# The second layer's modulation vectors: multiplied and summed on VectorE instead of TensorE, in a two-layer diffusion trunk

## Chip, cores and metric

One core of a Trainium2 chip runs the whole program. The metric is device time in microseconds (us) of one execution. Three runs of the kernel before took 1745.84 us at the median (1744.97 to 1749.46). About 0.3% of that, 5.2 us, is what a measurement can tell from no change.

## What is computed

The reference is a trunk of two layers over 256 latent tokens and 256 context tokens of width 1024. In every layer a conditioning vector (one for the latents, one for the context) gives six vectors of width 1024 that shift, scale and gate the tokens:

```python
silu_c, silu_cc = jax.nn.silu(c)[:, None, :], jax.nn.silu(c_ctx)
for i in range(DEPTH):                                   # DEPTH = 2
    m_lat = jnp.split(silu_c @ mod_w[i] + mod_b[i], 6, axis=-1)    # mod_w[i]: 1024 x 6144
    m_ctx = jnp.split(silu_cc @ mod_w[i] + mod_b[i], 6, axis=-1)
    # mixer: pooling | Hyena | differential attention, gated by m_lat[2], m_ctx[2]
    # layer 0: dense SwiGLU on both streams; layer 1: top-2 of 8 experts, latents only
```

So each layer's modulation is the product of a 1024 x 6144 matrix with two vectors. In the second layer the context stream is used only through its first two vectors (shift and scale of the first norm), since the result is the latent stream alone.

## The kernel before

The program runs in stages: loads and the first layer's modulation, the first mixer with its output projection, the dense SwiGLU of the first layer ("the dense stage"), the second mixer, and the routed experts.

**Modulation.** `mod_w` of a layer is cut into 12 tiles `ct` of 512 output columns, and each tile into 4 chunks `q` of 256 rows, loaded as a 128 x 1024 tile `modw` (L345). `modulation_part` (L353) multiplies a chunk on TensorE: the stationary operand is `cvec`, 128 x 32, which holds the two conditioning vectors (the other columns are 0), the moving operand is a 128 x 256 piece of the weights, and four such matmuls, for two row blocks and two column halves, stand side by side in the array. After the fourth chunk, `modulation_row` copies the sum to SBUF on ScalarE (L360), transposes it with two matmuls (L363), and VectorE adds the two halves (L367) and the bias (L369) into `modT`.

The first 10 tiles are done in the early stages. The last two tiles of layer 0 and the 12 tiles of layer 1, 14 x 4 = 56 chunks, are handed out one at a time by `mod_chunk`, as filler in the dense stage.

**The dense stage.** `dense` runs over 22 blocks of hidden width 128. Each takes two projections (gate and up) of 24 matmuls with 512 moving columns: `three` (L272 to L274) multiplies in three parts, since weights and activations are each split into a high and a low half. Calls of `mod_chunk` stand after each projection in `up`, and after each output block in the two first calls of `down`. "Block" below means one such set of 24 matmuls, of a projection or of a down-projection.

**Weights.** `weight` loads a 128 x 1024 tile `raw` (L259), ScalarE makes the high half `wh` (L262), VectorE the low half `wl` (L263). `raw` and `modw` share one ring of 7 buffers; `wh` and `wl` have 4 each. The projections write to one of three PSUM banks `mm`; for each pair ScalarE takes SiLU of one (L890), VectorE multiplies by the other (L891) and makes the low half of the product (L267). For an output block VectorE adds the two gated residuals (L839).

**Order of the work.** The program is written in the order of these loops; a scheduler then sets the order of each engine's queue, and each engine works through its own queue in order. All loads here go through SyncE's queue.

Of the kernel before, what the change touches and what calls it, by code (L numbers as in the profile page):

```python
# [18 lines left out]
F32 = mybir.dt.float32  # L19
# [3 lines left out]
OP = mybir.AluOpType  # L23
AX = mybir.AxisListType

P = 128
D = 1024
KD = D // P
L = 256
# [8 lines left out]
PAD = 8  # L38
# [157 lines left out]
class Trunk:  # L196
# [130 lines left out]
    def conditioning(self):  # L327

        nc = self.nc
        lo = self.par_at["c"][0]  # L330
        both = self.pars[:, lo:lo + 2 * KD]
        sc = self.keep.tile([P, 2 * KD], F32, name="silu_c")
        nc.scalar.activation(sc, both, AF.Exp, scale=-1.0)
        nc.vector.tensor_scalar(sc, sc, 1.0, None, op0=OP.add)
        nc.vector.reciprocal(sc, sc)
        nc.vector.tensor_mul(sc, sc, both)
        self.cvec = self.pre.tile([P, KD, 32], F32, name="cvec")
        nc.gpsimd.memset(self.cvec, 0.0)
        for j in range(2):
            nc.vector.tensor_copy(self.cvec[:, :, j], sc[:, j * KD:(j + 1) * KD])  # L340
# [51 lines left out]
    def mod_chunk(self):  # L392

        if not self.chunks:
            return
        l, ct, q = self.chunks.pop(0)
        if q == 0:
            self.mod_ps = self.sc()
        self.modulation_part(self.mod_ps, q, self.modulation_load(l, ct, q))
        if q == 3:  # L400
            self.modulation_row(l, ct, self.mod_ps, self.aux)

    def mod_chunks_until(self, l, ct):
        while self.chunks and self.chunks[0][:2] < (l, ct):
            self.mod_chunk()
# [1038 lines left out]
```

## Time and profile before

| | |
|---|---|
| median of 3 runs | 1745.84 us (1744.97 to 1749.46) |
| the profiled execution | 1746.36 us, its span 1743.9 us |
| TensorE busy | 1672.5 us (96%) |
| VectorE busy | 608.8 us (35%) |
| ScalarE busy | 444.2 us (25%) |
| GpSimd busy | 29.4 us (2%) |
| mean granted TensorE clock | 0.991 |

The span runs from the first instruction to the last; 2.46 us of the execution's time lie around it. PE is TensorE's matmul side, PEld its weight loads, DVE VectorE, ACT ScalarE, POOL GpSimd, SP SyncE. A record's duration is from its start to its modelled end; matmuls are pipelined, so the cost of one in a row of them is the distance from start to start. A float32 matmul shows as two records, one of the split halves (fp32r) and a transpose as one.

### The profile page before, as it was taken

The numbers are of one execution on the slowest core, as the hardware profiler recorded it, in microseconds if no ns is written. First come the engines' busy times: TensorE is split into PE (matmuls) and PEld (weight loads), VectorE is DVE, ScalarE is ACT, GpSimd is POOL, SyncE is SP. The second block draws the span as 40 slices with busy tenths as digits, with TensorE's granted clock in tenths as the row PEclk, the third lists the DMA queues.
The fourth block names the chain that finished last, engine by engine and source line by source line (L and its number), as shares of the span: only waits on it lengthen the run. The fifth ranks groups of instructions, "written<-read, shape, count | busy, mean of one in ns | idle before, by whom it ended". The sixth has DMA issues, their size and how long they took to land. (4 is left out here: it accounts for less than half of the span.)

```text
span 1743.9 us, 27710 instructions
## 1 busy us (share of the span) xinstructions
PE 1672.5 (96%) x11718; PEld 1107.2 (63%) x11718; DVE 608.8 (35%) x1352; ACT 444.2 (25%) x866; POOL 29.4 (2%) x38
## 2 busy tenths in 40 slices
PE   6999999999999999999979999999999999999977
PEld 3777568877777777887755555555555555556533
DVE  5645785533332333768740110221103111031103
ACT  4444464422122122546620100110001000010101
POOL 0021000000000000011000000000000000000000
PEclk8999999999999999999989999999999999999999
DMA  8531262455555554532549999999999999999995
GB/s 302 179 107 58 84 255 73 158 157 169 169 164 165 160 165 132 181 109 85 194 166 387 394 390 423 425 382 422 414 402 426 423 424 408 425 424 425 425 425 239
DMA packets 86314, 475.92 MB, mean 273 GB/s; under 512 B 9708, under 2 KB 13069, under 8 KB 43149
## 3 DMA queue, kind: packets, MB, share of 16 engines
q1 hardware_dynamic: 85580, 473.12, 70.4%
q8 instruction: 121, 1.98, 0.4%
q10 hardware_dynamic: 576, 0.52, 0.1%
q14 instruction: 37, 0.30, 0.1%
HBM read 472.55 MB, written 1.05 MB: 272 GB/s over the span
## 5 line engine op out<-in xcount | busy, mean ns | idle before, releaser
L1136 PE MATMUL mm<-mraw,xg 128*64 128x256 f32 x3584 | 407.8, 381 | 16.4 <-DMA mraw<-in_eg_dram 6.7
L1136 PEld LDWEIGHTS mm<-mraw,xg 128*64 128x64 f32 x3584 | 277.9, 137 | 152.8 <-issue 30.3
L272 PE MATMUL mm<-xh,wh 128*128 128x512 f32 (+1 forms) x656 | 240.8, 368 | 0.8 <-ACT wh L262 0.4
L274 PE MATMUL mm<-xh,wl 128*128 128x512 f32 (+1 forms) x656 | 237.6, 363 | 0.3 <-DVE wl L263 0.3
L273 PE MATMUL mm<-xl,wh 128*128 128x512 f32 (+1 forms) x656 | 237.6, 363 | 0.1
L262 ACT CAST wh<-raw 128x1024 fp32r<-128x1024 f32 (+1 forms) x124 | 128.0, 1034 | 362.6 <-PE mm L273 342.4
L263 DVE TENSOR_TENSOR wl<-raw,wh 128x1024 fp32r<-128x1024 f32 (+1 forms) x124 | 149.9, 1211 | 139.8 <-ACT wh L262 138.1
L1153 DVE TENSOR_TENSOR h<-h,mm 128x256 f32<-128x256 f32 x56 | 23.6, 421 | 408.2 <-ACT h L1152 408.1
L272 PEld LDWEIGHTS mm<-xh,wh 128*128 128x128 f32 x656 | 122.9, 188 | 37.0 <-issue 16.5
L274 PEld LDWEIGHTS mm<-xh,wl 128*128 128x128 f32 x656 | 123.2, 188 | 22.0 <-issue 2.2
L273 PEld LDWEIGHTS mm<-xl,wh 128*128 128x128 f32 x656 | 123.1, 188 | 18.9 <-issue 1.5
L1152 ACT ACTIVATE h<-mm 128x256 f32<-128x256 f32 x56 | 21.5, 383 | 415.7 <-PE mm L1136 415.6
L1185 PE MATMUL sc<-mraw,ht 128*64 128x512 f32 x448 | 109.1, 603 | 3.9 <-PEq L1192 1.9
L1185 PE MATMUL mm<-mraw,ht 128*64 128x512 f32 x448 | 108.8, 603 | 3.4 <-DMA mraw<-in_ed_dram 1.5
L1156 DVE TENSOR_TENSOR hx<-hx,sc 64x256 f32<-64x256 f32 x56 | 23.8, 425 | 232.0 <-ACT hx L1155 231.9
L1155 ACT ACTIVATE hx<-sc 64x256 f32<-64x256 f32 x56 | 21.0, 375 | 259.3 <-PE sc L1147 165.5
L1147 PE MATMUL sc<-mraw,xg 128*32 128x256 f32 x1344 | 76.4, 379 | 0.0
L1185 PEld LDWEIGHTS sc<-mraw,ht 128*64 128x64 f32 x448 | 28.9, 136 | 56.3 <-issue 39.4
L1185 PEld LDWEIGHTS mm<-mraw,ht 128*64 128x64 f32 x448 | 29.1, 136 | 52.1 <-issue 42.3
L1147 PEld LDWEIGHTS sc<-mraw,xg 128*32 128x32 f32 x1344 | 43.4, 110 | 29.5 <-issue 1.2
L839 DVE SCALAR_TENSOR_TENSOR x_latents<-mm,modT,x_latents 128x256 f32<-128x256 f32 x40 | 18.6, 481 | 95.7 <-PE mm L274 95.7
L353 PE MATMUL sc<-modw,cvec 128*32 128x256 f32 x576 | 45.0, 396 | 3.0 <-DMA modw<-in_mod_dram 2.9
(330 smaller groups left out, 2004.2 us busy)
## 6 DMA issues: line engine op xcount, KB each, us to landing
mraw<-in_eg_dram SPq DMA_DIRECT2D x112, 1024.0 KB, 14.4
mraw<-in_eu_dram SPq DMA_DIRECT2D x112, 1024.0 KB, 17.9
mraw<-in_ed_dram SPq DMA_DIRECT2D x112, 1024.0 KB, 11.1
modw<-in_mod_dram SPq DMA_DIRECT2D x96, 512.0 KB, 3.8
raw<-in_win_dram SPq DMA_DIRECT2D x40, 512.0 KB, 4.0
raw<-in_fg_dram SPq DMA_DIRECT2D x22, 512.0 KB, 4.6
raw<-in_fu_dram SPq DMA_DIRECT2D x22, 512.0 KB, 4.5
raw<-in_wout_dram SPq DMA_DIRECT2D x16, 512.0 KB, 4.2
```

The source lines that it names most:

```text
L262: nc.scalar.copy(hi, raw)
L263: nc.vector.tensor_sub(lo, raw, hi.bitcast(F32))
L272: mm(ps, w[0], x[0], start=start, stop=False)
L273: mm(ps, w[0], x[1], start=False, stop=False)
L274: mm(ps, w[1], x[0], start=False, stop=stop)
L353: self.nc.tensor.matmul(ps[g:g + 32, :L], self.cvec[:, 2 * q + k], w[:, k * 512 + n * L:k * 512 + (n + 1) * L], start=q == 0, stop=q == 3, ...
L1136: last = mm(pm[MAIN * j:MAIN * (j + 1), i * L:(i + 1) * L], xg[:, k, :MAIN], r, start=k == 0, stop=k == KD - 1, tile_position=(0, MAIN * j))
L1147: mm(px[q:q + EXTRA], xg[:, k, MAIN:], r, start=k == 0, stop=k == KD - 1, tile_position=(0, q))
L1152: nc.scalar.activation(h, pm[:, :L], AF.Silu)
L1153: nc.vector.tensor_mul(h, h, pm[:, L:])
L1156: nc.vector.tensor_mul(hx[64:], hx[64:], px[64:])
L1185: mm(pds[e % 2][n * MAIN:(n + 1) * MAIN], ht[:, c:c + MAIN], r[:, at + n * 512:at + (n + 1) * 512], start=ft == 0 and k == 0, stop=ft == N ...
```

## The change

For layer 1 a chunk no longer goes to TensorE. VectorE multiplies each 128 x 512 half of the chunk by the conditioning value of its row (one value a partition, `silu_c`) and adds it to a running sum: `pz` for the latents, `pa` for the context. The first operation of a tile is a `tensor_scalar` (L421 of the new file), the others are `scalar_tensor_tensor` (L423). For tiles `ct` 0 to 3, which hold shift and scale of the first norm, both streams are summed, for `ct` 4 to 11 the latents alone. After the fourth chunk TensorE sums over the partitions: for each 128 columns of a running sum one matmul with that 128 x 128 piece as the stationary operand and a column of ones as the moving one (L428). VectorE then adds the bias (L433). The tiles `pz` and `pa` take the place of tiles of the same names that the first mixer uses, with one buffer each. Layer 0's chunks stay as they were.

```diff
         nc.vector.tensor_mul(sc, sc, both)
+        self.silu_c = sc
...
         l, ct, q = self.chunks.pop(0)
+        if l == 1:
+            return self.mod_sums(ct, q)
         if q == 0:
             self.mod_ps = self.sc()
...
+    def mod_sums(self, ct, q):
+
+
+        nc = self.nc
+        streams = 2 if ct < 4 else 1
+        if q == 0:
+            wide = [self.temps.tile([P, 2, L + 2 * PAD], F32, name=self.name(n), tag=n, bufs=1) for n in ("pz", "pa")[:streams]]
+            self.sums = [t.rearrange("p s t -> p (s t)")[:, :512] for t in wide]
+        w = self.modulation_load(1, ct, q)
+        for k in range(2):
+            wk = w[:, k * 512:(k + 1) * 512]
+            for j, acc in enumerate(self.sums):
+                c = j * KD + 2 * q + k
+                c = self.silu_c[:, c:c + 1]
+                if q == k == 0:
+                    nc.vector.tensor_scalar(acc, wk, c, None, op0=OP.mult)
+                else:
+                    nc.vector.scalar_tensor_tensor(acc, wk, c, acc, op0=OP.mult, op1=OP.add)
+        if q == 3:
+            ps = self.aux(8)
+            for j, acc in enumerate(self.sums):
+                for b in range(4):
+                    nc.tensor.matmul(ps[:, 4 * j + b:4 * j + b + 1], acc[:, b * P:(b + 1) * P], self.ones[:, 0:1],
+                                     start=True, stop=True)
+            m, mb = self.modT[1][:, 4 * ct:4 * ct + 4], self.par("mod_b1")[:, 4 * ct:4 * ct + 4]
+            for j in range(2):
+                at = 4 * j if streams == 2 else 0
+                nc.vector.tensor_add(m[:, :, j], ps[:, at:at + 4], mb)
```

Three places show how the queues move. The first is TensorE's queue in the dense stage at the end of the first layer-1 tile. Before (`sc` is the bank of the chunks' sum, `aux` that of the transposes, `mm` those of the blocks; xN counts equal instructions):

```order
L273 MATMUL mm_3465<-xl_2647,wh_3461 128x512
L274 MATMUL mm_3465<-xh_2646,wl_3462 128x512
L353 MATMUL sc_3364<-modw_3490,cvec 32x256 x4
L272 MATMUL mm_3510<-xh_2632,wh_3506 128x512
L273 MATMUL mm_3510<-xl_2633,wh_3506 128x512
L274 MATMUL mm_3510<-xh_2632,wl_3507 128x512
L272 MATMUL mm_3510<-xh_2634,wh_3506 128x512
L363 MATMUL aux_3498<-tab_ident,t_710_3496 128x128 x2
L273 MATMUL mm_3510<-xl_2635,wh_3506 128x512
```

The same place in the change:

```order
L273 MATMUL mm_3466<-xl_2647,wh_3462 128x512
L274 MATMUL mm_3466<-xh_2646,wl_3463 128x512
L428 MATMUL aux_3497<-tab_ones,pz_3364 128x1 x4
L428 MATMUL aux_3497<-tab_ones,pa_3365 128x1 x4
L272 MATMUL mm_3514<-xh_2632,wh_3510 128x512
L273 MATMUL mm_3514<-xl_2633,wh_3510 128x512
```

The group of four at the end of every block is gone and so are the two transposes; eight matmuls with one moving column stand behind the fourth block of a tile (four where only the latents are summed), between the last matmul of one block and the first of the next.

The second place is VectorE's queue in the change around the end of that tile's sums and the start of the next tile's (L368 and L370 are the last row of layer 0, L923 is L891 of the file before):

```order
L423 SCALAR_TENSOR_TENSOR pa_3365<-modw_3491,silu_c,pa_3365 128x512
L263 TENSOR_TENSOR wl_3463<-raw_3460,wh_3462 128x1024
L368 TENSOR_REDUCE modT_73<-aux_3327 128x4 x2
L370 TENSOR_TENSOR modT_73<-modT_73,pars 128x8
L923 TENSOR_TENSOR t_690_3372<-t_690_3372,mm_3339 128x512
L263 TENSOR_TENSOR wl_3511<-raw_3508,wh_3510 128x1024
L267 TENSOR_TENSOR v_692_3376<-t_690_3372,v_691_3375 128x512
L263 TENSOR_TENSOR wl_3557<-raw_3554,wh_3556 128x1024
L923 TENSOR_TENSOR t_703_3453<-t_703_3453,mm_3422 128x512
L263 TENSOR_TENSOR wl_3594<-raw_3591,wh_3593 128x1024
L267 TENSOR_TENSOR hy_705_3457<-t_703_3453,hy_704_3456 128x512
L421 TENSOR_SCALAR pz_3539<-modw_3541,silu_c 128x512
```

The last addition to the first tile's sums stands ahead of `wl_3463`, the weights of the block `mm_3466` behind which TensorE sums. The first operation of the next tile writes `pz` again and so stands behind TensorE's sums; ahead of it are the weights of the three blocks that follow those sums.

The third place is VectorE's queue in the first down-projection, where both streams are summed beside the residuals (L871 is L839 of the file before):

```order
L871 SCALAR_TENSOR_TENSOR x_latents<-mm_3691,modT_73,x_latents 128x256
L871 SCALAR_TENSOR_TENSOR x_context<-mm_3691,modT_73,x_context 128x256
L423 SCALAR_TENSOR_TENSOR pz_3716<-modw_3796,silu_c,pz_3716 128x512
L423 SCALAR_TENSOR_TENSOR pa_3717<-modw_3796,silu_c,pa_3717 128x512
L423 SCALAR_TENSOR_TENSOR pz_3716<-modw_3796,silu_c,pz_3716 128x512
L423 SCALAR_TENSOR_TENSOR pa_3717<-modw_3796,silu_c,pa_3717 128x512
L263 TENSOR_TENSOR wl_3807<-raw_3804,wh_3806 128x1024
L423 SCALAR_TENSOR_TENSOR pz_3716<-modw_3835,silu_c,pz_3716 128x512
L871 SCALAR_TENSOR_TENSOR x_latents<-mm_3732,modT_73,x_latents 128x256
L871 SCALAR_TENSOR_TENSOR x_context<-mm_3732,modT_73,x_context 128x256
```

Four multiply-adds stand between the residuals of one block and the next, where before there was only one `wl`. SyncE's queue holds the same loads in the same order as before.

## Rows read from the trace of the kernel before

**Rows 1.** Page, part 1: busy time of TensorE, share, instructions
```profile
PE 1672.5 (96%) x11718; PEld 1107.2 (63%) x11718; DVE 608.8 (35%) x1352; ACT 444.2 (25%) x866; POOL 29.4 (2%) x38
```
**Rows 2.** Windows: length, busy time (instructions) of each engine, clock, DMA share, GB/s
```profile
core 0: us, PE busy (x) PEld busy (x) DVE busy (x) ACT busy (x) POOL busy (x), PEclk, DMA share, GB/s
340.00:380.00 40.00, 40.00 (x201) 29.99 (x200) 13.43 (x20) 11.49 (x15) 0.00 (x0) 1.00 0.47 143
...
660.00:700.00 40.00, 40.00 (x190) 30.82 (x189) 14.23 (x26) 10.77 (x18) 0.00 (x0) 1.00 0.44 129
700.00:850.00 150.00, 144.81 (x805) 114.38 (x803) 115.37 (x244) 85.85 (x170) 12.39 (x16) 1.00 0.44 150
...
1000.00:1200.00 200.00, 196.90 (x1838) 111.82 (x1836) 31.10 (x79) 20.95 (x50) 0.00 (x0) 1.00 0.99 407
...
1400.00:1600.00 200.00, 195.96 (x1738) 113.56 (x1732) 31.39 (x82) 21.63 (x52) 0.00 (x0) 1.00 1.01 421
```
**Rows 3.** Timeline of TensorE in the dense stage, one chunk to the next: start, duration
```profile
384.20 0.39 PE L274 MATMUL mm<-xh,wl 128*128 128x512 f32 x1
384.52 0.64 PE L353 MATMUL sc<-modw,cvec 128*32 128x256 f32 x8
...
385.67 0.39 PE L274 MATMUL mm<-xh,wl 128*128 128x512 f32 x1
385.90 0.39 PE L272 MATMUL mm<-xh,wh 128*128 128x512 f32 x1
...
390.48 0.40 PE L274 MATMUL mm<-xh,wl 128*128 128x512 f32 x1
390.80 0.64 PE L353 MATMUL sc<-modw,cvec 128*32 128x256 f32 x8
```
**Rows 4.** The same timeline around the two transposes of a tile
```profile
398.45 0.40 PE L272 MATMUL mm<-xh,wh 128*128 128x512 f32 x1
398.68 0.38 PE L363 MATMUL aux<-tab_ident,t 128*128 128x128 f32 x2
...
399.37 0.39 PE L272 MATMUL mm<-xh,wh 128*128 128x512 f32 x1
```
**Rows 5.** Groups by line, TensorE, 340 to 705 us: records, busy, mean ns, idle
```profile
L353 PE MATMUL sc<-modw,cvec 128*32 128x256 f32 x416 | 33.2, 391 | 0.0
```
**Rows 6.** Timeline of TensorE, filter stage: matmuls with one moving column (L475)
```profile
64.20 0.95 PE L475 MATMUL sc<-tab_ones,t 128*128 128x1 f32 x8
65.01 0.68 PE L485 MATMUL sc<-k,tab_st 128*128 128x256 f32 x2
```
**Rows 7.** Timeline of TensorE's weight loads at the same place
```profile
63.98 1.08 PEld L475 LDWEIGHTS sc<-tab_ones,t 128*128 128x128 f32 x8
64.98 0.30 PEld L485 LDWEIGHTS sc<-k,tab_st 128*128 128x128 f32 x2
```
**Rows 8.** All records of that line: duration in ns, minimum, median, maximum
```profile
L475 PE MATMUL sc<-tab_ones,t x32: 167/260/372, 30.7 to 64.9; 128*128 128x1 f32 x32
```
**Rows 9.** Groups by line, VectorE, 0 to 340 us
```profile
L622 DVE SCALAR_TENSOR_TENSOR e<-e,st 128x512 f32<-128x512 f32 x8 | 5.9, 743 | 0.0
...
L621 DVE TENSOR_SCALAR e<-e,st 128x512 f32<-128x512 f32 x8 | 3.9, 484 | 0.1
...
L663 DVE TENSOR_TENSOR hy<-hy,hy 128x512 f32<-128x512 f32 x2 | 2.3, 1138 | 0.0
```
**Rows 10.** Groups by line, VectorE, 340 to 705 us
```profile
L263 DVE TENSOR_TENSOR wl<-raw,wh 128x1024 fp32r<-128x1024 f32 x51 | 62.5, 1225 | 74.4 <-ACT wh L262 72.7
L891 DVE TENSOR_TENSOR t<-t,mm 128x512 f32<-128x512 f32 x20 | 13.7, 687 | 83.2 <-PE mm L274 83.2
L839 DVE SCALAR_TENSOR_TENSOR x_latents<-mm,modT,x_latents 128x256 f32<-128x256 f32 x21 | 10.2, 484 | 76.3 <-PE mm L274 76.3
```
**Rows 11.** Page, part 6: the chunks' loads, median us from issue to landing
```profile
modw<-in_mod_dram SPq DMA_DIRECT2D x96, 512.0 KB, 3.8
```
**Rows 12.** Window of the filter stage, columns as in rows 2
```profile
60.00:68.00 8.00, 7.95 (x48) 6.44 (x47) 3.06 (x11) 2.54 (x7) 0.00 (x0) 1.00 0.40 149
```

## The prediction

> **What bounds the kernel now.** I read the page's busy times first: TensorE is busy for 96% of the span, VectorE for 35% [rows 1]. The share says little of what an edit is worth, so next I cut the span into stretches [rows 2]. In the dense stage (340 to 700 us) TensorE is busy for all of every 40 us, at a granted clock of 1.00 (the 2.4 GHz level), while VectorE works 13.4 to 14.2 us of 40, ScalarE 11, GpSimd nothing, and the DMA engines stand at about 0.45. So in this stage an instruction that leaves TensorE's queue takes its whole distance from the time, if the others keep up. The second mixer (700 to 850 us) is not so clear-cut, and the experts behind it move 407 to 421 GB/s at a DMA share of 0.99 to 1.01: the loads bound them. All of layer 1's chunks lie in the dense stage, so the change acts there, and the later stages should only start earlier.
>
> **What leaves TensorE.** A record's duration overlaps with the next, so I take distances from start to start. Within a block, 385.90 to 390.48 us is 20 steps: 0.229 us each [rows 3]. From the last matmul of one block (384.20) to the third of the next (385.67) it is 1.47 us where three steps would be 0.69, so a chunk's group costs 0.78 us. The period from group to group says the same: 6.28 us less 24 x 0.229 = 5.50 leaves 0.78 [rows 3]. The stretch holds 416 such records with no idle time before them, eight to a chunk [rows 5], that is 52 of the 56 chunks; 48 of them are layer 1's. The two transposes of a tile: 398.45 to 399.37 us is 0.92 us for three steps, so 0.23 us more [rows 4]. Removed: 48 x 0.784 = 37.6 us and 12 x 0.233 = 2.8 us, together 40.4 us. ScalarE loses 12 small copies, VectorE the two reduces and the addition of each tile; neither was on the path.
>
> **What comes to TensorE.** Four tiles with two streams take 8 matmuls each, eight tiles with one stream take 4: 64 matmuls, 128 records. The filter stage has the very same form, a 128 x 128 float32 stationary piece and one moving column [rows 6]: eight records (four matmuls) from 64.20 to the next operation's start at 65.01 us, 0.81 us. Their weight loads run from 63.98 to 64.98 us, 1.00 us, one behind the other [rows 7]: the load, not the column, is what is paid. In the dense stage the next block's first load queues behind these, so I take 1.00 us for eight records; 16 sets of eight are 16.0 us. The ends: 0.81 us gives 13.0 us, if the edges hide; the median record of that line, 260 ns [rows 8], laid end to end gives 33.3 us. Durations overlap in a row of matmuls, as they do for the chunks, so I stay near the low end. The Trainium skill ("TensorE: Matmul & The Clock Gate", section on LDWEIGHTS) speaks against this form: it says that a load takes its columns divided by 1.2 in ns however little is multiplied, which for 128 columns is 107 ns. By that figure, as an estimate, the 128 records cost 13.7 us and the total comes 2.3 us lower; the trace's 125 ns per load includes what lies between them, and decides.
>
> The net on TensorE is 40.4 - 16.0 = 24.4 us less (7.1 to 27.4 between the ends).
>
> **What comes to VectorE.** The nearest rows are attention's 128 x 512 operations, float32 in SBUF with a value per partition: 743 ns for a multiply-add, 484 ns for a multiply [rows 9]. A two-stream tile takes 2 x 0.484 + 14 x 0.743 = 11.4 us, a one-stream tile half: 4 x 11.4 + 8 x 5.7 = 91 us more on an engine that is idle two thirds of this stage. The additions of the bias are as small as the three operations that they replace. Cover, block by block: with the group gone a block takes TensorE 5.50 us, and a two-stream tile adds 2.0 us of sums to four blocks: 6.0 us. VectorE then has 11.4/4 = 2.84 us of sums, one low half at 1.225, and either half of a pair's two operations at 0.69 (0.69 us a block) or two residuals at 0.48 [rows 10]: 4.8 to 5.0 us of 6.0. With one stream it is 3.3 to 3.6 us of 5.75. So it fits, tightly for the first 16 chunks. A first tile's `pz` write waits until TensorE is past the sums of the tile before, and holds up what is queued behind it. By the queue in the change, the weights of three blocks (16.5 us of TensorE) stand ahead of it, and the next weights, `wl_3638`, come after 2 multiplies, 10 multiply-adds, a product and its low half, some 10 us, and 1.2 us of their own. That is 11 us against 16.5. The last addition to a tile stands ahead of the weights of the block behind which the sums are taken, so TensorE should not wait for the sums either. I cost VectorE's part at nothing on the path; if the cover is gone, the next block's `wl` is what is late.
>
> **Loads.** SyncE's queue holds the same loads. A chunk's buffer now comes free when VectorE has used it, which is several blocks ahead of where TensorE used it; a chunk lands 3.8 us after its issue [rows 11], and the same bytes now move in a stage that is 7% shorter, from a DMA share of 0.45 or so. I count nothing.
>
> **The sum.** The profiled execution took 1746.36 us, 0.5 us over the median of the three runs. 1746.36 - 24.4 = 1722.0 us. The ends of the sums' price give 1719 and 1739 us.
>
> **Rivals.**
>
> *VectorE becomes the bound while both streams are summed.* For it: 5.0 of 6.0 us. A two-input product of the same size took 1138 ns in one place [rows 9]. At that price four operations are 4.55 us, a block 6.7 us against 6.0, and 16 blocks lose some 12 us: 1734 us. Against it: that product ran in the first mixer; GpSimd works in a mixer (12.4 us in the second) and does nothing in the dense stage [rows 2], and the multiply-adds themselves took 743 ns [rows 9]. Chance 0.10.
>
> *The gain is swallowed later.* For it: the experts run at the rate of their loads [rows 2]; if those were issued by a clock of their own, an earlier dense stage would only make TensorE wait longer. Against it: the DMA share in the second mixer is 0.44, so the loads do not run on through it; their buffers come free only as the stages before end. It would give 1746 us, no change. Chance 0.05.
>
> *The queues wait on each other, and it is slower.* TensorE stands at each tile's sums, because the last multiply-adds wait for a chunk that was issued only after TensorE's own progress. The price for a tile is the landing of a load, 3.8 us [rows 11], and the last 4 (or 2) multiply-adds, 3.0 (1.5) us: 4 x 6.8 + 8 x 5.3 = 69.6 us, net 45 us more, 1792 us. It loses from 24.4/12 = 2.0 us of standing per tile on. For it speaks that VectorE's queue cannot be overtaken, so one late load holds up low halves too. The Trainium skill says so as a rule ("TensorE: Matmul & The Clock Gate", table at the head): VectorE's queue is strictly first in, first out, while TensorE may pull weight loads forward. By that rule alone any late chunk costs TensorE; no row of the kernel before can show it for these chunks, as VectorE did not read them. Against the rival: in the changed queue a tile's last addition precedes the weights of a block that TensorE has yet to run before the sums. Chance 0.05.
>
> *The one-column matmuls cost the clock.* They hardly fill the array. Against it: in the window that holds two such sets of eight the granted clock is 1.00 [rows 12]. Chance 0.02; one such fall per tile of a few us at half speed would take back most of the gain, so I count it as no change.
>
> **How the numbers follow.** The forecast, 1722 us, has 0.78; VectorE as the bound 0.10; swallowed 0.05; the clock 0.02; slower 0.05. Faster by over 0.3% (5.2 us, about what a measurement of this kernel can tell from no change) are the first two, 0.88. No change within 0.3%: 0.07. Slower: 0.05. The range: below, 1719 us and the 4.5 us over which the three runs spread, so 1715; above, VectorE's case at 1734 and a little more, 1736, which leaves out the dearest price of the sums, the unchanged and the slower cases.
>
> **What would show it.** In the profile of the changed kernel: 128 records of L428 in the dense stage, some 1.0 us per eight from the block before to the block after; blocks 5.5 us apart; TensorE still fully busy with clock 1.00 and VectorE at 70 to 80% in the first third of the stage and 55% later; multiply-adds at 0.74 us; the stretch from the dense stage's end to the program's end as long as before. Wrong would be: idle time of TensorE in front of L428 for a VectorE sum or in front of L274 for `wl`; multiply-adds over 1 us; or an unchanged end in spite of a dense stage that ends 24 us sooner.

## The result and the profile after

The changed kernel took 1720.1 us at the median of four runs (1718.63 to 1721.62), the kernel before 1747.65 us (1744.97 to 1749.79) beside it: a ratio of 0.9843 with a 95% interval of 0.9824 to 0.9862, faster by some 27.5 us. The profiled execution has a span of 1717.9 us where before it was 1743.9, 26.0 us less.

The page's busy times of the kernel after, which answer to [rows 1]:

```profile
PE 1648.3 (96%) x11438; PEld 1115.2 (65%) x11438; DVE 688.1 (40%) x1468; ACT 441.1 (26%) x854; POOL 29.4 (2%) x38
```

TensorE's share stayed at 96%: it lost 24.2 us of work and the span lost 26.0. Where in the program they went is read from the first and the last SiLU of the dense stage, two marks that both kernels have. ScalarE's timeline before (start, duration):

```profile
324.36 1.08 ACT L890 ACTIVATE t<-mm 128x512 f32<-128x512 f32 x2
...
678.11 0.61 ACT L890 ACTIVATE t<-mm 128x512 f32<-128x512 f32 x1
```

The same two in the kernel after:

```profile
322.03 1.09 ACT L922 ACTIVATE t<-mm 128x512 f32<-128x512 f32 x2
...
649.95 0.59 ACT L922 ACTIVATE t<-mm 128x512 f32<-128x512 f32 x1
```

Up to the first mark: 324.4 and 322.0 us, 2.4 less. Between the marks, the dense stage: 353.7 and 327.9, 25.8 less. From the last mark to the end of the span: 1065.8 and 1067.9, 2.1 more. So the whole gain lies in the dense stage, and the two other differences nearly cancel. The windows of the kernel after show what they are (columns as in [rows 2]):

```profile
0.00:100.00 100.00, 83.89 (x493) 60.75 (x494) 55.71 (x140) 46.58 (x87) 0.64 (x8) 0.97 0.65 229
...
340.00:380.00 40.00, 40.00 (x197) 30.54 (x196) 23.89 (x37) 10.76 (x15) 0.00 (x0) 1.00 0.60 189
420.00:460.00 40.00, 40.00 (x181) 32.49 (x181) 33.21 (x55) 7.35 (x7) 0.00 (x0) 1.00 0.58 175
...
780.00:860.00 80.00, 72.34 (x419) 53.44 (x418) 57.38 (x139) 44.70 (x105) 4.08 (x5) 0.94 0.48 184
1000.00:1200.00 200.00, 196.43 (x1836) 111.44 (x1836) 32.02 (x85) 20.77 (x50) 0.00 (x0) 1.00 0.99 409
```

In the dense stage TensorE is busy for all of every 40 us at a granted clock of 1.00, as before, and VectorE works up to 33.2 us of 40 where it worked 12 to 14. The first 100 us were granted 0.97, where the kernel before has 0.93:

```profile
0.00:100.00 100.00, 83.66 (x483) 60.75 (x484) 55.00 (x140) 46.57 (x87) 0.64 (x8) 0.93 0.65 229
```

The second mixer was granted 0.94 between 780 and 860 us; the same work lay some 28 us later before, and 808 to 888 us have 0.98 there. Both differences turn up in runs below whose edits leave those parts alone: the first SiLU stood at 321.6 to 322.0 us in runs with 0.97 at the start and at 323.8 to 324.7 in those with 0.93 to 0.95, and the stretch behind the last SiLU took 1064.5 us in two kernels with this change and 1067 to 1069 in the others. So either end of the program scatters by some 3 to 5 us from run to run, and an edit is best judged by the length of the dense stage.

TensorE's timeline after, at the end of the first tile of layer 1, with both streams:

```profile
392.08 0.39 PE L274 MATMUL mm<-xh,wl 128*128 128x512 f32 x1
392.31 0.95 PE L428 MATMUL aux<-tab_ones,pz 128*128 128x1 f32 x8
393.12 1.03 PE L428 MATMUL aux<-tab_ones,pa 128*128 128x1 f32 x8
394.01 0.48 PE L272 MATMUL mm<-xh,wh 128*128 128x512 f32 x1
394.33 0.40 PE L273 MATMUL mm<-xl,wh 128*128 128x512 f32 x1
394.57 0.39 PE L274 MATMUL mm<-xh,wl 128*128 128x512 f32 x1
```

From one L274 to the next is 2.49 us where three steps of 0.229 are 0.69: sixteen records cost 1.80 us. In the last tile, with one stream, the same reading gives 0.91 us for eight:

```profile
648.97 0.39 PE L274 MATMUL mm<-xh,wl 128*128 128x512 f32 x1
649.20 0.95 PE L428 MATMUL aux<-tab_ones,pz 128*128 128x1 f32 x8
...
650.57 0.39 PE L274 MATMUL mm<-xh,wl 128*128 128x512 f32 x1
```

So all sums cost 4 x 1.80 + 8 x 0.91 = 14.5 us, and 40.4 us left: 25.9 us net, where the stage became 25.8 shorter. What VectorE did in the stage (322 to 655 us, groups by line as in [rows 9, 10]):

```profile
L263 DVE TENSOR_TENSOR wl<-raw,wh 128x1024 fp32r<-128x1024 f32 x55 | 66.9, 1221 | 26.1 <-ACT wh L262 25.0
L423 DVE SCALAR_TENSOR_TENSOR pz<-modw,silu_c,pz 128x512 f32<-128x512 f32 x84 | 62.8, 748 | 3.1 <-DMA modw<-in_mod_dram 2.0
L423 DVE SCALAR_TENSOR_TENSOR pa<-modw,silu_c,pa 128x512 f32<-128x512 f32 x28 | 20.9, 745 | 0.0
...
L421 DVE TENSOR_SCALAR pz<-modw,silu_c 128x512 f32<-128x512 f32 x12 | 5.7, 479 | 11.0 <-PE aux L428 7.8 <-DMA modw<-in_mod_dram 3.2
```

The new operations lasted 748 and 479 ns, 91 us in all with the 1.9 us of `pa`'s multiplies. But one starts before the record of the one ahead of it ends, so VectorE's busy time on the page rose by only 79.3 us, from 608.8 to 688.1. VectorE's wait for TensorE's sums in the same stretch (engine, line, what it waited for: us in total, times, longest):

```profile
DVE modT L433 <- PE aux L428: 26.4, 12, 4.2
```

And TensorE's, the whole list:

```profile
PE mm L272 <- ACT t L922: 0.4, 1, 0.4
```

VectorE stands behind TensorE's sums, as its place in the queue makes it; TensorE stands for nothing of VectorE's.

### The profile page after: what moved, and what is told of

Same layout as the page of the kernel before. It is cut to its first block, busy times and chain, and to the rows that moved or that the text cites. A ratio compares the mean times of both kernels' runs of the same rounds, so it can differ in the third digit from the quotient of the medians.

```text
span 1717.9 us, 27274 instructions
## 1 busy us (share of the span) xinstructions
PE 1648.3 (96%) x11438; PEld 1115.2 (65%) x11438; DVE 688.1 (40%) x1468; ACT 441.1 (26%) x854; POOL 29.4 (2%) x38
## 5 line engine op out<-in xcount | busy, mean ns | idle before, releaser
L274 PE MATMUL mm<-xh,wl 128*128 128x512 f32 (+1 forms) x656 | 237.8, 363 | 0.3 <-DVE wl L263 0.3
L274 PEld LDWEIGHTS mm<-xh,wl 128*128 128x128 f32 x656 | 123.1, 188 | 21.8 <-issue 2.2
L1184 ACT ACTIVATE h<-mm 128x256 f32<-128x256 f32 x56 | 21.5, 383 | 414.5 <-PE mm L1168 414.5
L423 DVE SCALAR_TENSOR_TENSOR pz<-modw,silu_c,pz 128x512 f32<-128x512 f32 x84 | 62.8, 748 | 3.1 <-DMA modw<-in_mod_dram 2.0
L643 PE MATMUL sc<-k,q 64*128 64x512 f32 (+1 forms) x96 | 40.0, 580 | 1.5 <-DVE k L632 1.0
```

Of the source, the lines that this page charges most:

```text
L274: mm(ps, w[1], x[0], start=False, stop=stop)
L423: nc.vector.scalar_tensor_tensor(acc, wk, c, acc, op0=OP.mult, op1=OP.add)
L643: nc.tensor.matmul(s[m], q[h][r, qs], k[h][r, k0:k0 + nk], start=True, stop=True)
```

## The experiments

The theory: the dense stage is TensorE's alone, so it shortens by what leaves TensorE less the price of the one-column sums, and VectorE's work is covered. Rivals to be told apart: VectorE is close to taking over, or the loads of the chunks are; the sums have a price besides their weight loads. In all edits below the lines are those of the changed kernel.

**One stream's tiles alone.** Tiles 0 to 3 go back to TensorE, so that a part of the sum is tried by itself.

```diff
-        if l == 1:
+        if l == 1 and ct >= 4:
             return self.mod_sums(ct, q)
```

> The changed kernel with the four two-stream tiles of layer 1 back on TensorE; only the eight one-stream tiles go through VectorE. If the time follows TensorE's queue alone, the gain is a sum over tiles: 8 x (4 x 0.784 + 0.233 - 0.91) = 19.7 us against the kernel before (0.91 us is what eight one-column records cost in the changed kernel's trace), so the dense stage from the first SiLU to the last is 353.7 - 19.7 = 334.0 us, and the whole 6 us above the changed kernel. If VectorE at 5 of 6 us in the two-stream tiles costs something there, those tiles gave less than their 6.2 us and this kernel comes within 3 us of the changed one.

The dense stage took 334.0 us, 19.7 less than in the kernel before, as the sum has it; the whole took 1725.11 us (ratio 0.9882, 0.9857 to 0.9906). A two-stream tile is worth (334.0 - 327.9)/4 = 1.5 us, and 3.37 us less its 1.80 of sums is 1.57. So the sum by tiles holds for both kinds of tile.

**The sums twice.** The one-column matmuls of each tile run two times over, with the same result.

```diff
-                for b in range(4):
+                for b in (0, 1, 2, 3, 0, 1, 2, 3):
                     nc.tensor.matmul(ps[:, 4 * j + b:4 * j + b + 1], acc[:, b * P:(b + 1) * P], self.ones[:, 0:1],
```

> Every matmul with one moving column is issued twice (128 more records, the same result). If these are paid in full on TensorE, at the 0.91 us per eight of the changed kernel's trace, the dense stage grows by 16 x 0.9 = 14.5 us, to 342.5 us, and at the 1.00 us that the prediction took by 16.0 us. If they stand in time that TensorE had to spend anyway, waiting for VectorE, it grows by less than 5 us.

Measured: a dense stage of 349.4 us, 21.5 more in place of 14.5; 1739.99 us (0.996, 0.9948 to 0.9973). The profiled execution is the longest of ten (1735.76 to 1744.91 us); the shortest lies 15.7 us over the median of the change, little more than the price, so the excess is not the same in every run. In the profiled one the 7 us over the price stand behind the two-stream tiles. TensorE's timeline at the first of them:

```profile
394.96 1.84 PE L428 MATMUL aux<-tab_ones,pz 128*128 128x1 f32 x16
396.67 2.26 PE L428 MATMUL aux<-tab_ones,pa 128*128 128x1 f32 x16
398.79 0.77 PE L272 MATMUL mm<-xh,wh 128*128 128x512 f32 x1
399.36 0.63 PE L273 MATMUL mm<-xl,wh 128*128 128x512 f32 x1
399.79 0.63 PE L274 MATMUL mm<-xh,wl 128*128 128x512 f32 x1
...
404.91 0.42 PE L274 MATMUL mm<-xh,wl 128*128 128x512 f32 x1
405.16 0.40 PE L272 MATMUL mm<-xh,wh 128*128 128x512 f32 x1
```

And windows at that place:

```profile
395.00:398.70 3.70, 3.70 (x33) 3.70 (x31) 0.48 (x1) 1.47 (x2) 0.00 (x0) 0.92 0.00 0
398.70:404.50 5.80, 5.80 (x16) 4.54 (x16) 5.26 (x10) 0.00 (x0) 0.00 (x0) 0.50 0.28 93
```

Behind 32 one-column records in a row the matmuls stand 0.43 us apart for 6 us, in place of 0.23, and the granted clock is 0.50, the 1.2 GHz level, though nothing was waited for. Behind the other three such runs the slow stretch is some 3.5 us long. The fourth rival's mechanism exists, then, at twice the length that the change has. The run of 32, or the doubled number?

**The same number, apart.** The added set of a tile stands two blocks ahead of the tile's own, on the identity, with its result unused.

```diff
         w = self.modulation_load(1, ct, q)
+        if q == 1:
+            more = self.aux(8)
+            for b in range(4 * streams):
+                nc.tensor.matmul(more[:, b:b + 1], self.ident, self.ones[:, 0:1], start=True, stop=True)
```

> As many one-column matmuls as in sums_twice (128 in place of 64), but the added set of a tile stands two blocks ahead of the tile's own sums, behind the second block, with the identity as its operand and its result unused, so that no more than 16 records follow each other. If the length of a run lowered the clock in sums_twice: the dense stage is longer than the change's 328.0 us by the price of the sums alone, 14.5 us, so 342.5 us, with a granted clock of 1.00 in every 40 us. If the number of such matmuls in the stretch lowered it: about 349 us again, as in sums_twice (349.4), with windows below 1.00 in the first 120 us of the stage. If a run of 16 is already at the edge: something between, with some windows below 1.00.

342.4 us, and 1736.03 us in all (0.9936, 0.9915 to 0.9957). The clock around the first pair:

```profile
383.00:388.00 5.00, 5.00 (x32) 4.40 (x31) 1.23 (x1) 1.54 (x2) 0.00 (x0) 1.00 0.26 86
...
395.80:398.00 2.20, 2.20 (x20) 2.11 (x19) 0.72 (x4) 1.54 (x2) 0.00 (x0) 1.00 0.03 7
398.00:404.00 6.00, 6.00 (x28) 4.93 (x27) 5.57 (x9) 0.85 (x1) 0.00 (x0) 1.00 0.35 101
```

The price of the sums is confirmed a second time, 14.5 us for as many again, and what lowered the clock was the run of 32 in a row, not their number. (The added sets have the identity as their operand; whether the data plays a part wasn't tried.)

**More streams on VectorE.** Both streams are summed in all twelve tiles, then three (the third repeats the first), and TensorE sums as many as in the change; what is added is VectorE's alone. The edit shown is the one for three; the one for two has `[:2]`.

```diff
-            wide = [self.temps.tile([P, 2, L + 2 * PAD], F32, name=self.name(n), tag=n, bufs=1) for n in ("pz", "pa")[:streams]]
+            wide = [self.temps.tile([P, 2, L + 2 * PAD], F32, name=self.name(n), tag=n, bufs=1) for n in ("pz", "pa", "pb")[:3]]
...
-                c = j * KD + 2 * q + k
+                c = j % 2 * KD + 2 * q + k
...
-            for j, acc in enumerate(self.sums):
+            for j, acc in enumerate(self.sums[:streams]):
```

With two:

> VectorE multiplies and sums both streams in all 12 tiles; TensorE sums the same pieces as in the changed kernel, and the context sums of the last eight tiles go unused. VectorE gets 8 x 5.7 = 45.5 us more, TensorE nothing. If VectorE is covered as long as its work for a block (2.97 + 1.22 + 0.69 to 0.96 = 4.9 to 5.2 us) stays under TensorE's 5.7, the dense stage stays at 328 us within 2. If its queue already costs time at that load, by waits that a sum of busy times does not show, it grows by 5 to 20 us.

With three:

> A third running sum in all 12 tiles, unused (it repeats the latents' stream). VectorE's work for a block becomes 6 x 0.746 + 1.22 + 0.69 to 0.96 = 6.4 to 6.7 us against TensorE's 5.7. If the price of VectorE's work is that of the longer of two covered queues, the 48 blocks with a chunk lose 0.7 to 1.0 us each: the dense stage grows by 30 to 45 us, to 358 to 373 us, and TensorE's idle time appears in front of its low-half matmuls (wl). If the two queues add up rather than cover each other, it grows by more than 100 us; if VectorE has more slack than the sum says, by less than 15.

Two: a dense stage of 327.9 us, as in the change, and 1720.46 us (0.9847, 0.9829 to 0.9865). Three: 329.7 us, 1.8 more, and 1723.63 us (0.9862, 0.9841 to 0.9884), where I had expected tens of us. VectorE with three:

```profile
540.00:580.00 40.00, 40.00 (x178) 32.54 (x177) 38.25 (x60) 8.97 (x10) 0.00 (x0) 1.00 0.57 183
```

And what TensorE waited for:

```profile
PE mm L272 <- ACT t L922: 0.6, 2, 0.4
PE mm L274 <- DVE wl L263: 0.4, 1, 0.4
```

VectorE filled 96% of some 40 us and TensorE stood 0.4 us for a low half. Why so little came of it, when this expectation has 6.4 to 6.7 us of VectorE's work for a block against 5.7 of TensorE's, its timeline shows:

```profile
545.52 0.74 DVE L423 SCALAR_TENSOR_TENSOR pz<-modw,silu_c,pz 128x512 f32<-128x512 f32 x1
546.18 0.74 DVE L423 SCALAR_TENSOR_TENSOR pa<-modw,silu_c,pa 128x512 f32<-128x512 f32 x1
...
549.50 1.21 DVE L263 TENSOR_TENSOR wl<-raw,wh 128x1024 fp32r<-128x1024 f32 x1
550.63 0.74 DVE L423 SCALAR_TENSOR_TENSOR pz<-modw,silu_c,pz 128x512 f32<-128x512 f32 x1
```

Six multiply-adds stand between 545.52 and 549.50 us: a record lasts 0.74 us, but the next starts 0.66 us after it, and behind a low half of 1.21 us the next starts after 1.13. From start to start six multiply-adds (3.98 us), a low half and 0.6 to 0.8 us for the rest are 5.7 to 5.9 us a block, and less in the first block of a tile, whose multiplies stand 0.40 us apart. That is about TensorE's 5.7. I had costed VectorE by durations, in the prediction and again in this expectation, though TensorE by distances; by distances three streams just fit, and two have 4.4 to 4.6 us. What the four buffers of low halves and the blocks without a chunk add to the cover wasn't tried.

**GpSimd at work.** Three additions of a 128 x 512 tile on GpSimd are put beside each chunk, to test the 1138 ns product of [rows 9].

```diff
         w = self.modulation_load(1, ct, q)
+        if q == 0:
+            self.other = self.temps.tile([P, 2, L + 2 * PAD], F32, name=self.name("pb"), tag="pb", bufs=1).rearrange("p s t -> p (s t)")[:, :512]
+            nc.gpsimd.memset(self.other, 0.0)
+        for _ in range(3):
+            nc.gpsimd.tensor_add(self.other, self.other, self.other)
```

> GpSimd gets three 128x512 additions on a tile of its own for each chunk of layer 1, 144 in all, which nobody reads. If the 1138 ns product of the mixer was slow because GpSimd worked at the same time, VectorE's multiply-adds beside such an addition last over 1 us (746 ns alone), the two-stream part becomes VectorE-bound and the dense stage grows by 5 to 20 us. If the two engines do not disturb each other, the multiply-adds stay at 0.75 us and the dense stage at 328 us.

1774.18 us (1.0149, 1.0129 to 1.0169), but in another place than meant: the additions need nothing of the chunk and ran ahead, in the first mixer. The first SiLU came at 377.3 us, the dense stage stayed at 327.9. The mixer's VectorE operations answer the question all the same (100 to 324 us, groups by line):

```profile
L652 DVE TENSOR_REDUCE st<-sc 128x1 f32<-128x512 f32 x16 | 10.9, 679 | 1.6 <-PE sc L648 1.6
...
L658 DVE TENSOR_SCALAR e<-e,st 128x512 f32<-128x512 f32 x8 | 8.9, 1110 | 0.1
...
L659 DVE SCALAR_TENSOR_TENSOR e<-e,st 128x512 f32<-128x512 f32 x8 | 8.2, 1022 | 0.0
...
L282 DVE TENSOR_SCALAR rv<-aux 128x512 f32<-128x512 f32 x10 | 6.8, 683 | 2.7 <-ACT ry L281 2.7
```

The change's own rows of the same operations:

```profile
L647 DVE TENSOR_REDUCE st<-sc 128x1 f32<-128x512 f32 x16 | 10.9, 684 | 4.5 <-PE sc L643 4.3
...
L282 DVE TENSOR_SCALAR rv<-aux 128x512 f32<-128x512 f32 x10 | 6.8, 683 | 4.1 <-ACT ry L281 4.1
...
L654 DVE SCALAR_TENSOR_TENSOR e<-e,st 128x512 f32<-128x512 f32 x8 | 6.0, 744 | 0.0
...
L653 DVE TENSOR_SCALAR e<-e,st 128x512 f32<-128x512 f32 x8 | 3.9, 484 | 0.1
```

Beside GpSimd the multiply goes from 484 to 1110 ns and the multiply-add from 744 to 1022, while operations that read their one large operand from PSUM (`sc`, `aux`) stay at 680. The 1138 ns product itself is settled by the trace of the kernel before. That figure is the mean of two:

```profile
119.73 1.30 POOL L736 TENSOR_TENSOR pd<-pb,tab_icnt 64x512 f32<-64x512 f32 x1
...
119.99 1.59 DVE L663 TENSOR_TENSOR hy<-hy,hy 128x512 f32<-128x512 f32 x1
...
145.58 0.69 DVE L663 TENSOR_TENSOR hy<-hy,hy 128x512 f32<-128x512 f32 x1
```

One stands beside a GpSimd operation and lasts 1.59 us, the other, with GpSimd idle, 0.69. The Trainium skill ("SBUF — State Buffer", section "Who interferes with whom") says that VectorE and GpSimd share one pair of SBUF ports, and that an operation with two SBUF inputs (beside a GpSimd operation that reads SBUF), or in a two-port mode, contends for it, and one with at most one SBUF input outside those modes does not. The rows of the product, the multiply-add and the readers of PSUM agree; whether the multiply, with one SBUF input, ran in such a mode no row shows.

**Five buffers in the ring.** `raw` and `modw` share five buffers in place of seven, in the change and in the kernel before.

```diff
-        raw = self.ring.tile([P, 1024], F32, name=self.name("raw"), tag="raw", bufs=7)[:, :n]
+        raw = self.ring.tile([P, 1024], F32, name=self.name("raw"), tag="raw", bufs=5)[:, :n]
...
-        w = self.ring.tile([P, 1024], F32, name=self.name("modw"), tag="raw", bufs=7)
+        w = self.ring.tile([P, 1024], F32, name=self.name("modw"), tag="raw", bufs=5)
```

In the change:

> The changed kernel with 5 buffers instead of 7 for the loaded weights and chunks. If loads are covered with room to spare, as the sum assumes, the dense stage stays at 328 us within 2. If VectorE's queue stands behind late chunks (a chunk lands 4.9 us after its issue), low halves come late: idle time of TensorE in front of wl, and 10 to 40 us more.

In the kernel before:

> The kernel before with 5 buffers instead of 7. There a chunk's buffer is held until TensorE has used it, several blocks after it landed. If the earlier release by VectorE is part of the gain, this kernel loses more than the changed kernel does with 5 buffers (its dense stage over 360 us against 353.7); if loads play no part in either, both stay where they are.

The change: a dense stage of 328.9 us, 1.0 more; 1730.08 us (0.9897, 0.9877 to 0.9916), the rest of it lost ahead of the stage, whose first SiLU came at 331.4 us. The kernel before: 362.3 us, 8.5 more; 1765.14 us (1.0097, 1.0077 to 1.0117). There TensorE waited 4.6 us for ScalarE's copies of the chunks' sums:

```profile
PE aux L363 <- ACT t L360: 4.6, 10, 0.8
```

Those are about half of the 8.5 us; where the rest went the list of waits doesn't show. So in the change the stage bears a shorter ring better, which fits a chunk's buffer that comes free sooner; with seven buffers neither kernel is short, and nothing of the gain comes from there.

**Layer 0's last tiles too.** Its tiles 10 and 11 go the same way, and then tile 11 alone.

```diff
-        if l == 1:
-            return self.mod_sums(ct, q)
...
+        return self.mod_sums(l, ct, q)
...
-    def mod_sums(self, ct, q):
+    def mod_sums(self, l, ct, q):
...
-        streams = 2 if ct < 4 else 1
+        streams = 2 if l == 0 or ct < 4 else 1
...
```

> The two tiles of layer 0 that the dense stage also holds go through VectorE too (both streams). TensorE loses 8 x 0.784 + 2 x 0.233 = 6.7 us and gets two sets of sixteen one-column records at 1.80 us, 3.6 us: 3.1 us less than the changed kernel, 1717 us. If the start of the dense stage, where VectorE still prepares the activations, has no room for 22.8 us more of VectorE work, the gain is gone or turns into a loss of a few us.

1724.76 us (0.987, 0.985 to 0.9891), no better than the change. The dense stage became shorter, 326.1 us (1.8 less than in the change, where 3.1 was expected), but began later: the first SiLU came at 327.7 us against 322.0, at the same 0.97 in the first 100 us. Tile 10's sums and tile 11's first operations stand among those that prepare the stage's activations; TensorE waited 1.2 us for one of these right behind a set of sixteen one-column records (311.78 to 313.6 us), and then ran at half the clock:

```profile
312.00:314.00 2.00, 1.62 (x15) 1.54 (x14) 1.44 (x5) 0.00 (x0) 0.00 (x0) 1.00 0.85 317
314.00:316.00 2.00, 1.19 (x5) 1.19 (x6) 2.00 (x6) 1.31 (x3) 0.00 (x0) 0.51 0.05 20
316.00:318.00 2.00, 2.00 (x12) 2.00 (x11) 2.00 (x6) 1.31 (x3) 0.00 (x0) 0.50 0.00 0
```

A longer wait, 2.25 us at 326 us, with no such records ahead of it, left the clock at 1.00, so a wait alone need not do it.

Tile 11 alone (against the edit above; tile 10 is back on TensorE by lines that are not shown):

```diff
-        return self.mod_sums(l, ct, q)
+        if (l, ct) != (0, 10):
+            return self.mod_sums(l, ct, q)
...
```

> Layer 0's tile 11 alone goes through VectorE beside layer 1's; tile 10, whose chunks stand at the start of the stage beside the activation's preparation, stays on TensorE. The tile removes 4 x 0.784 + 0.233 = 3.37 us from TensorE and adds sixteen records at 1.80 us: 1.6 us less, 326.4 us of dense stage in place of 328.0. If the two tiles of layer0_too delayed the start of the stage only by the work of tile 10, the first SiLU stands where it does in the change (322 us at a clock of 0.97 in the first 100 us) and the total is some 1718.5 us, a difference of 0.1% that hardly shows in the total. If VectorE is too full there even for tile 11, the first SiLU comes later by 1 us or more and nothing is left of it.

A dense stage of 326.4 us, as the sum has it, with the first SiLU at 324.4 us and 0.93 at the start, where the kernel before has it too. 1718.28 us (0.9837, 0.9814 to 0.986): 1.8 us under the change, which its total can't tell from nothing, though the stage shows 1.5 us of it.

## Why the prediction was right

The forecast was 1722.0 us and 1720.1 was measured, by the mechanism that was forecast: the gain is the dense stage's, by what left TensorE's queue less the price of the sums. That the total agrees so well is in part luck, since the two other differences, 2.4 us less ahead of the stage and 2.1 more behind it, scatter from run to run as shown above and happen to cancel. Point by point:

- **What leaves TensorE, 40.4 us.** It held. The stage lost 25.8 us where this sum and the measured price of the sums give 25.9, and the one-stream kernel confirms it by tiles.
- **What comes to TensorE, 16.0 us.** Somewhat too dear: 14.5 us. I took 0.125 us per load from the filter stage's eight loads, but in the dense stage sixteen records cost 1.80 us and eight 0.91, 0.113 us each. The Trainium skill's 107 ns per load ("TensorE: Matmul & The Clock Gate", section on LDWEIGHTS) gave 13.7 us as an estimate. The measurement lies between the two, nearer to the figure of the Trainium skill. The record's own duration, 260 ns, which made the upper end, is no price in a row of matmuls.
- **What comes to VectorE, 91 us covered.** Covered, yes: 748 and 479 ns where 743 and 484 were taken, and no wait of TensorE for it. But 91 us is a sum of durations, and the engine's busy time rose by 79. From start to start a multiply-add costs 0.66 us, so a two-stream block has 4.4 to 4.6 us of VectorE's work and not 4.8 to 5.0, and the cover is wider than I worked out. VectorE's share, forecast at 70 to 80% in the first third, was 60% between 340 and 380 us and 83% between 420 and 460.
- **Loads, nothing.** The median landing of a chunk rose to 4.9 us from [rows 11]'s 3.8, and no wait of TensorE came of it. The DMA share of the whole stage was 0.54 before, not 0.45: the two rows that I took it from are the lowest of the stage.
- **The rivals.** The 1138 ns of the first was no price of any one operation but the mean of 1.59 us beside GpSimd and 0.69 without, and GpSimd does nothing in the dense stage; no run put work on GpSimd beside the multiply-adds of the sums. The later stages swallowed nothing: the experts ran as before, at 409 GB/s. The queues did not wait on each other: VectorE waits for TensorE's sums, not the reverse. The clock was kept, but with less room than the 0.02 said: twice the run lowers it, and so does a run of the same length with a short wait behind it.

## What to carry to other kernels

Where one engine is busy without a gap, cost what leaves its queue from start to start of its neighbours, and judge the edit by the length of that stage between two marks that both kernels have, since totals scatter by more than small terms. Cost the engine that takes over the work in the same way: its records overlap too (0.74 us long, 0.66 apart), and a sum of durations makes it look fuller than it is. Such an engine can be filled nearly to the brim: here 96% of 40 us cost TensorE next to nothing. Before taking a mean of two records as a price, look at both and at what ran beside them. Keep runs of matmuls with one moving column short, and keep them away from places where TensorE will wait.

## What the runs showed of the hardware that I had not expected

- 32 one-column records in a row (3.5 to 3.8 us, TensorE shown as busy throughout) were followed by 3.5 to 6 us at the 1.2 GHz level, with matmuls 0.43 us apart, behind each of the four such runs of the profiled execution; 16 in a row (1.80 us) were not, except where a wait of 1.2 us stood right behind them. The Trainium skill ("TensorE: Matmul & The Clock Gate", "What's actually happening") says that the gate follows how busy TensorE has been. Here the trace's busy column is full and the clock fell all the same, so that column is no guide to it; why, these runs don't settle.
- Work on GpSimd more than doubles a simple multiply on VectorE between SBUF tiles (484 to 1110 ns) and a product of two (0.69 to 1.59 us), and leaves alone what reads PSUM (683 and 683 ns).
- VectorE's records overlap like TensorE's: 128 x 512 multiply-adds in a row last 0.74 us and start 0.66 us apart.
